# The start of an attention kernel on one core: warm-up matmuls of ones, one K half copied by DMA, odd keys turned earlier, and new numbers in its planner

## The chip, the cores and the metric

One core of one Trainium2 chip. The time is device time of one execution in microseconds (us); medians over several executions are quoted. The span of a profile is from the first to the last recorded instruction; where the same execution was timed, the time is 1.8 us above the span.

## The reference

Grouped-query attention: 8 batches, 8 query heads over 2 key/value heads, 1024 positions, head size 64, all in float32.

```python
scores = scale * np.matmul(q_group, k_group.transpose(0, 1, 3, 2))
attn = np.exp(scores - scores_max)
attn = attn / (np.sum(attn, axis=-1, keepdims=True) + 1e-08)
output[:, q_start:q_end, :, :] = np.matmul(attn, v_group)
```

## The kernel before

A job is 512 queries of one head; it has eight cells of 128 keys by 512 queries. For each cell TensorE makes a 128x512 score tile. ScalarE exponentiates most of them, two tiles at a time (`aps` to `pa`); VectorE does the rest with bit arithmetic (`dps` to `pd`). TensorE then multiplies by V. A planner (`make_plan`) simulates the engines when the program is built and fixes the order of everything. Even and odd keys sit in two halves (parity), and K is stored with zeros in the other 64 rows (side), so that one Q tile of 128 rows serves both jobs of a head. To turn a tile means to transpose it, which TensorE does here.

The first head cannot use the transposing transfers of later ones, and is prepared by hand:

```python
last_score[0] = keep_warm(WARM)              # 26 matmuls of zeros
for n, half in enumerate(halves):
    nc.scalar.copy(out=hk[:, half, 0:2, :], in_=fk[:, half])
    nc.vector.tensor_copy(out=hq[:, half], in_=...)
    turn_k(0, half)                          # two transposes: even keys
    keep_warm(2)
    ...                                      # two transposes of Q
    keep_warm(2)
...
for half in halves:
    nc.scalar.copy(out=qT[(0, 0)][:, cols], in_=tq[:, cols])
    put_k(0, 0, half)                        # VectorE: PSUM to K
def second():                                # at 0.45 us of the plan: after three scores
    turn_k(1, every)                         # four transposes: odd keys
    for side, parity in ((0, 1), (1, 0), (1, 1)):
        put_k(side, parity, every)
nc.vector.tensor_copy(out=hk[:, :, 2, :], in_=fk[:, :, 0, :])
at(SECOND, second)
```

The exponential, 411 times on ScalarE:

```python
nc.scalar.activation(out=pt[:, 0:m], in_=psum.pop(("A", n))[:, 0:m], func=AF.Exp, scale=scale)
```

The softmax here doesn't subtract the row's maximum and nothing guards it: scores larger than these inputs give would overflow.

Of the kernel before, what the change touches and what calls it, by code (L numbers as in the profile page):

```python
# [12 lines left out]
CURVE_A, CURVE_B = 0.32988085, -0.33401025  # L13

GROUP = 8
POOL_STEP = -1


def make_plan(nj, nkc):
# [5 lines left out]


    QK, PV, P1, NORM = 0.216, 0.1225, 0.603, 0.555
    EXP, AND, LINE, PRODUCT = (0.065, 0.4265), (0.20, 0.133), (0.20, 0.133), (0.16, 0.27)
    CHAIN = (AND, LINE, PRODUCT, PRODUCT)
    FROM_PE, FROM_ACT, FROM_DVE, FROM_POOL = 0.26, 0.17, 0.10, 0.15  # L30
    LIVE_A, LIVE_D, PENDING, PER_JOB, LEAD, RAMP, AHEAD, FIRST_PV = 28, 5, 16, 2, 6, 3, 0.08, 2.0
    INF = 1e9
    FIRST_LOAD, EACH_LOAD = 3.5, 4.0
    ops = []
    pe = act = dve = 0.0
    a_free, bank, obank_free = [0.0, 0.0], [0.0, 0.0], [0.0, 0.0]
# [18 lines left out]
    while normed < nj:  # L55
# [9 lines left out]
        if job_a < nj:  # L65
            t = INF
# [21 lines left out]
        for q, p, kind in ((normq, 0, "norm"), (p1q, 1, "p1"), (chainq, 2, "chain")):  # L88
            if q:
                at = q[0][0]  # L90
                if kind != "chain" or q[0][3] != POOL_STEP:
                    at = max(dve, at)
                best = min(best or (INF,), (at, p, kind, 0))
        if cur and job_d >= nj and not p1q:
# [2 lines left out]
        if kind == "qk":  # L97
            t = best[4]
            pe = t + QK
            j = job_d if arg else job_a  # L100
            cell = j * nkc + todo[j].pop(0)
            if not arg:
                if open_a is None:
                    slot = first_free(a_free)
                    a_id += 1
                    live["A"] += 1
                    open_a = {"slot": slot, "t": a_free[slot], "cells": []}
                    a_free[slot] = INF
                o = open_a
                ops.append((t, "qk", cell, "A", a_id, o["slot"], len(o["cells"])))  # L110
                o["cells"].append(cell)
                home[cell] = ("A", a_id)
                if len(o["cells"]) == 2 or not any(todo[job_a:]):
                    act = max(act, pe + FROM_PE)
                    ops.append((act, "exp", a_id, tuple(o["cells"])))
                    act += EXP[0] + EXP[1] * len(o["cells"])
                    a_free[o["slot"]] = act + FROM_ACT
                    uses[("A", a_id)] = len(o["cells"])
                    for x in o["cells"]:
                        ready[x] = act + FROM_ACT  # L120
                    open_a = None
            else:
                taken[j] += 1
                k = first_free(bank)
                bank[k] = INF
                pending += 1
                ops.append((t, "qk", cell, "D", k, 0, 0))
                p1q.append((pe + FROM_PE, cell, k))
        elif kind == "open":
            o = first_free(obank_free)  # L130
            obank[arg] = o
            obank_free[o] = INF
            open_jobs.append(arg)
            rem[arg] = list(range(nkc))
            next_job += 1
        elif kind == "pv":
            s, c = arg
            cell = s * nkc + c
            opens = len(rem[s]) == nkc
            rem[s].remove(c)  # L140
            done = not rem[s]
            ops.append((t, "pv", s, cell, opens, done, obank[s]))
            pe = t + PV
            h = home[cell]
            uses[h] -= 1
            if not uses[h]:
                live[h[0]] -= 1
            if done:
                open_jobs.remove(s)
                normq.append((pe + FROM_PE, s))  # L150
        elif kind == "norm":
            s = normq.pop(0)[1]
            ops.append((t, "norm", s))
            dve = t + NORM
            obank_free[obank[s]] = dve + FROM_DVE
            normed += 1
        elif kind == "p1":
            _, cell, k = p1q.pop(0)
            if not cur:
                d_id += 1  # L160
                live["D"] += 1
            ops.append((t, "p1", cell, k, d_id, len(cur)))
            dve = t + P1
            bank[k] = dve + FROM_DVE
            cur.append(cell)
            home[cell] = ("D", d_id)
            if len(cur) == GROUP:
                chainq.append((dve, d_id, cur, 0))
                cur = []
        elif kind == "flush":  # L170
            chainq.append((dve, d_id, cur, 0))
            cur = []
        else:
            _, g, cells, step = chainq.pop(0)
            ops.append((t, "chain", g, len(cells), step))
            end = t + CHAIN[step][0] + CHAIN[step][1] * len(cells)
            dve = end if step != POOL_STEP else dve
            if step + 1 < len(CHAIN):
                at = end + FROM_POOL if step == POOL_STEP else end
                at += FROM_DVE if step + 1 == POOL_STEP else 0.0  # L180
                chainq.insert(0, (at, g, cells, step + 1))
            else:
                pending -= len(cells)
                uses[("D", g)] = len(cells)
                for x in cells:
                    ready[x] = dve + FROM_DVE
# [4 lines left out]
def kernel(  # L191
# [25 lines left out]
    NQS = QBS // 128  # L217
    E1 = D + 1
    PIECE = 256
    WARM = 26  # L220
    SECOND = 0.45
    CAST_GAP = 3.0
    scale = 1.0 / math.sqrt(D)
    bits_scale = 128.0 * scale * math.log2(math.e)
    bits_bias = 128.0 * 127.0
# [4 lines left out]

    jobs = [(b, h, side) for b in range(B) for h in range(H) for side in range(2)]
    plan = make_plan(len(jobs), NKC)

    const_pool = ctx.enter_context(tc.tile_pool(name="constp", bufs=1))
    scr_pool = ctx.enter_context(
# [19 lines left out]
    apools, dbanks, obanks = psum_pools("aps", 2), psum_pools("dps", 2), psum_pools("ops", 2)  # L255

    blank = const_pool.tile([128, 128], BF16)
    nc.vector.memset(blank, 0.0)  # L258
    ident = const_pool.tile([128, 128], BF16)
    make_identity(nc, ident)  # L260
    vsets, ksets = [], []
# [11 lines left out]

    def at(t, f, *args):
        events.append((t, len(events), f, args))

    qT = {}
    kT = {}
# [49 lines left out]
    def first_loads():  # L328
# [46 lines left out]
        for n, half in enumerate(halves):  # L375
            nc.scalar.copy(out=hk[:, half, 0:2, :], in_=fk[:, half])  # L376
            nc.vector.tensor_copy(
                out=hq[:, half], in_=fq[:, half].rearrange("p c two d -> p c (two d)")
            )
            turn_k(0, half)  # L380
            keep_warm(2)
            for c in range(NHC)[half]:
                nc.tensor.transpose(tq[:, c * 128 : (c + 1) * 128], hq[:, c, :], ident)  # L383
            keep_warm(2)
            if n == 0:
                cast(("q", 0, 2), q[0, 2])
        for half in halves:
            cols = slice(half.start * 128, half.stop * 128)
            nc.scalar.copy(out=qT[(0, 0)][:, cols], in_=tq[:, cols])  # L389
            put_k(0, 0, half)  # L390
        def second():
            every = slice(0, NHC)
            turn_k(1, every)
            for side, parity in ((0, 1), (1, 0), (1, 1)):
                put_k(side, parity, every)

        nc.vector.tensor_copy(out=hk[:, :, 2, :], in_=fk[:, :, 0, :])
        at(SECOND, second)

    p_of = {}  # L400
    psum = {}
# [43 lines left out]

    def exp_curve(g, m, step):
        pd = groups[g][:, 0:m]
        if step == 0:
            z = tmp_pool.tile([128, GROUP, QBS], U16, name="z")[:, 0:m]
            temps[g] = [z]  # L450
            nc.vector.tensor_scalar(  # L451
                out=z, in0=pd, scalar1=0x7F, scalar2=None, op0=ALU.bitwise_and
            )
        elif step == 1:
            y = tmp_pool.tile([128, GROUP, QBS], FP16, name="y")[:, 0:m]
            temps[g].append(y)
            nc.vector.tensor_scalar(  # L457
                out=y,
                in0=temps[g][0],
                scalar1=CURVE_A / 128.0,  # L460
# [3 lines left out]
            )  # L464
        elif step == 2:
            z, y = temps[g]
            nc.vector.tensor_tensor(out=y, in0=z, in1=y, op=ALU.mult)  # L467
        else:
            y = temps.pop(g)[1]
            groups.pop(g)  # L470
            nc.vector.tensor_tensor(out=pd, in0=pd, in1=y, op=ALU.add)  # L471

    def output_mms(s, cell, opens, closes, bk):
        b, h, side = jobs[s]
# [13 lines left out]
    def normalise(s):  # L488
# [1 line left out]
        o = ops_of.pop(s)  # L490
        rec = recip_pool.tile([128, NQS], FP32, name="rec")
        nc.vector.reciprocal(out=rec, in_=o[:, :, D])  # L492
        if side == 0:
            stage[(b, h)] = ostage_pool.tile([128, NQS, 2, D], FP32, name="ost")
        nc.vector.tensor_tensor(  # L495
            out=stage[(b, h)][:, :, side, :],
# [9 lines left out]
            in_=stage[(b, h)][:, :, sides],  # L506
        )

    first_use = {}
    run = {"qk": score, "exp": exps, "p1": exp_bits, "chain": exp_curve,  # L510
           "pv": output_mms, "norm": normalise}
    for op in plan:
        if op[1] == "qk":
            first_use.setdefault(op[2] // (2 * NKC), op[0])
        elif op[1] == "norm":
            b, h, side = jobs[op[2]]
            if op[2] >= len(jobs) - 2:
                at(op[0] + 0.01, put_out, b, h, slice(side, side + 1))
            elif side:
                at(op[0] + 1.5, put_out, b, h, slice(0, 2))  # L520
        at(op[0], run[op[1]], *op[2:])

# [4 lines left out]
    for b in range(B):  # L527
        for h in range(H):
# [8 lines left out]
            if h % HPG == 0:  # L537
# [4 lines left out]
                    at(th - 11.0 - 15.0 * spare + n, transpose_k, b, g, n)  # L542
                for side in range(2):
                    for parity in range(2):
                        at(th - 6.0 - 9.0 * spare, place_k, b, g, side, parity)
                for two in range(2):
                    at(th - 4.0 - 8.0 * spare + two, place_v, b, g, two)
    casts.sort(key=lambda e: e[0])
    latest = 1e9
    for n in reversed(range(len(casts))):  # L550
# [3 lines left out]
    for t, key, src in casts:  # L554
        t = max(t, soonest)
        soonest = t + 2.0
        at(t, cast, key, src)
    with tc.manual_schedule():
        first_loads()
        for _, _, f, args in sorted(events, key=lambda e: e[:2]):  # L560
# [31 lines left out]
```

## Time and profile before

| | before |
|---|---|
| median time, 3 executions | 393.41 us (393.38 to 393.47) |
| the profiled execution: span, and its own time | 393.7 us, 395.51 us |
| ScalarE busy | 380.7 us (97%) |
| fourth exponential starts | 13.30 us |
| last exponential ends; last normalisation ends; span ends | 388.33; 389.81; 393.70 us |

The prediction below shows the lines that carry this and how to read them. In the timeline a row is start, duration, engine, line, what was written from what, how many were merged, and in brackets the idle time before and what ended it.

### The profile page before, as it was taken

The numbers are of one execution on the slowest core, as the hardware profiler recorded it, in microseconds if no ns is written. First come the engines' busy times: TensorE is split into PE (matmuls) and PEld (weight loads), VectorE is DVE, ScalarE is ACT, GpSimd is POOL, SyncE is SP. The second block draws the span as 40 slices with busy tenths as digits, with TensorE's granted clock in tenths as the row PEclk, the third lists the DMA queues.
The fourth block names the chain that finished last, engine by engine and source line by source line (L and its number), as shares of the span: only waits on it lengthen the run. The fifth ranks groups of instructions, "written<-read, shape, count | busy, mean of one in ns | idle before, by whom it ended". The sixth has DMA issues, their size and how long they took to land.

```text
span 393.7 us, 12506 instructions
## 1 busy us (share of the span) xinstructions
PE 371.0 (94%) x5166; PEld 234.3 (60%) x5166; DVE 366.2 (93%) x573; ACT 380.7 (97%) x416; POOL 107.1 (27%) x184
## 2 busy tenths in 40 slices
PE   7989999999999999999999999999999999999995
PEld 5435556566666566566566566566556556556664
DVE  3799999999999999999999999999999999999992
ACT  4799999999999999999999999999999999999994
POOL 4285241413205032141413305032331416000000
PEclk9999999999999999999999999999999999999999
DMA  7499995756959559394665868468595658520113
GB/s 120 87 169 203 140 142 101 148 80 126 156 100 148 109 111 148 91 156 86 123 107 116 143 117 132 105 115 134 103 133 105 130 87 148 101 72 28 55 55 82
DMA packets 101992, 45.39 MB, mean 115 GB/s; under 512 B 66256, under 2 KB 99536, under 8 KB 100688
## 3 DMA queue, kind: packets, MB, share of 16 engines
q0 software_dynamic: 21600, 17.05, 34.9%
q1 hardware_dynamic: 79792, 27.29, 30.5%
q8 instruction: 40, 0.66, 0.7%
q10 hardware_dynamic: 544, 0.26, 0.2%
q14 instruction: 16, 0.13, 0.1%
HBM read 25.17 MB, written 27.00 MB: 133 GB/s over the span
## 4 chain that ended last, share of the span: by engine, by line
ACT 81%; PE 11%; issue 6%; DMA 1%; DVE 0%
ACT pa L427 80%; PE aps L416 5%; PE ops L479 4%; PE dps L416 2%; DMA fk<-in_k_dram 1%; DVE kset L350 0%; PE dps L341 0%; ACT qT L389 0%; PE ops L368 0%; PE dps L383 0%; DVE ost L495 0%; ACT hk L376 0%; DVE rec L492 0%
## 5 line engine op out<-in xcount | busy, mean ns | idle before, releaser
L427 ACT ACTIVATE pa<-aps 128x1024 bf16<-128x1024 f32 x411 | 378.0, 1064 | 3.9 <-PE aps L416 3.8
L416 PE MATMUL aps<-qT,kset 128*128 128x512 bf16 x822 | 245.8, 380 | 15.8 <-ACT pa L427 13.8
L479 PEld LDWEIGHTS <-pa 128*128 128x128 bf16 x3288 | 137.6, 98 | 61.1 <-issue 1.1
L479 PE MATMUL ops<-vset,pa 128*128 128x65 bf16 x3288 | 149.1, 194 | 0.0
L436 DVE TENSOR_SCALAR pd<-dps 128x512 uint16<-128x512 f32 x202 | 130.9, 682 | 3.7 <-PE dps L416 3.1
L416 PEld LDWEIGHTS <-kset 128*128 128x128 bf16 x1024 | 82.6, 98 | 73.4 <-issue 37.4
L286 POOL DMA_DIRECT2D scr_q<-in_q_dram x63 | 34.4, 545 | 201.5 <-PE aps L416 152.2
L416 PE MATMUL dps<-qT,kset 128*128 128x512 bf16 x202 | 71.4, 383 | 1.2 <-DVE kset L350 0.9
L495 DVE TENSOR_TENSOR ost<-ops,rec 128x256 f32<-128x256 f32 x128 | 54.3, 424 | 4.4
L471 DVE TENSOR_TENSOR pd<-pd,y 128x4096 uint16<-128x4096 uint16 (+1 forms) x26 | 57.8, 2224 | 0.3
L467 DVE TENSOR_TENSOR y<-z,y 128x4096 f16<-128x4096 uint16 (+1 forms) x26 | 57.7, 2220 | 0.1
L479 PEld LDWEIGHTS <-pd 128*128 128x128 bf16 x808 | 36.5, 97 | 18.3 <-DVE pd L471 0.6
L479 PE MATMUL ops<-vset,pd 128*128 128x65 bf16 x808 | 41.3, 193 | 0.0
L306 POOL DMA_DIRECT2D kset<-kT x60 | 34.5, 584 | 1.4 <-issue 0.4
L457 DVE TENSOR_SCALAR y<-z 128x4096 f16<-128x4096 uint16 (+1 forms) x26 | 31.5, 1210 | 0.0
L451 DVE TENSOR_SCALAR z<-pd 128x4096 uint16<-128x4096 uint16 (+1 forms) x26 | 31.3, 1202 | 0.0
L492 DVE RECIPROCAL rec<-ops 128x4 f32<-128x4 f32 x128 | 22.6, 176 | 9.0 <-PE ops L479 7.7
L319 POOL DMA_DIRECT2D vset<-in_v_dram x32 | 26.4, 831 | 2.1 <-issue 1.9
L286 POOL DMA_DIRECT2D scr_k<-in_k_dram x15 | 8.1, 540 | 28.1 <-PE aps L416 22.2
L368 PE MATMUL ops<-blank 128*128 128x128 bf16 x34 | 4.6, 312 | 1.0 <-DVE blank L258 1.0
L368 PEld LDWEIGHTS <-blank 128*128 128x128 bf16 x34 | 3.7, 148 | 1.0 <-DVE blank L258 1.0
L350 DVE COPY kset<-dps 64x512 bf16<-64x512 bf16 (+1 forms) x5 | 1.7, 365 | 2.8 <-PE dps L341 2.7
(19 smaller groups left out, 12.6 us busy)
## 6 DMA issues: line engine op xcount, KB each, us to landing
out_dram<-ost SPq DMA_DIRECT2D x63, 256.0 KB, 3.2
scr_q<-in_q_dram POOLq DMA_DIRECT2D x63, 128.0 KB, 3.2
kset<-kT POOLq DMA_DIRECT2D x60, 64.0 KB, 3.4
vset<-in_v_dram POOLq DMA_DIRECT2D x32, 64.0 KB, 4.9
qT<-scr_q SPq DMA_TRANSPOSE x126, 4.0
scr_k<-in_k_dram POOLq DMA_DIRECT2D x15, 128.0 KB, 3.2
kset<-kset POOLq DMA_DIRECT2D x6, 128.0 KB, 4.9
kT<-scr_k SPq DMA_TRANSPOSE x30, 4.0
```

Source lines behind the costliest of these rows:

```text
L286: dma = nc.gpsimd.dma_start(out=scr.rearrange("(p f) -> p f", f=1024), in_=src.rearrange("(p s) d -> p (s d)", s=1024 // D),)
L306: nc.gpsimd.dma_start(out=ksets[b % 2][side * D : (side + 1) * D, g, side, parity * HALF : (parity + 1) * HALF], in_=kT[(b, g)][parity * D ...
L319: nc.gpsimd.dma_start(out=vsets[b % 2][:, g, two * NHC : (two + 1) * NHC, 0:D], in_=v[b, g].rearrange("(c p two) d -> two p c d", p=128, t ...
L416: last_score[0] = nc.tensor.matmul(dst, lhsT=ksets[b % 2][:, h // HPG, side, c * 128 : (c + 1) * 128], rhs=qT[(b, h)], start=True, stop=Tr ...
L427: nc.scalar.activation(out=pt[:, 0:m], in_=psum.pop(("A", n))[:, 0:m], func=AF.Exp, scale=scale)
L436: nc.vector.tensor_scalar(out=groups[g][:, slot], in0=psum.pop(cell), scalar1=bits_scale, scalar2=bits_bias, op0=ALU.mult, op1=ALU.add,)
L451: nc.vector.tensor_scalar(out=z, in0=pd, scalar1=0x7F, scalar2=None, op0=ALU.bitwise_and)
L457: nc.vector.tensor_scalar(out=y, in0=temps[g][0], scalar1=CURVE_A / 128.0, scalar2=CURVE_B, op0=ALU.mult, op1=ALU.add,)
L467: nc.vector.tensor_tensor(out=y, in0=z, in1=y, op=ALU.mult)
L471: nc.vector.tensor_tensor(out=pd, in0=pd, in1=y, op=ALU.add)
L479: nc.tensor.matmul(ops_of[s][:, qs, :], lhsT=p_of[cell][:, qs * 128 : (qs + 1) * 128], rhs=vsets[b % 2][:, h // HPG, c, :], start=opens an ...
L495: nc.vector.tensor_tensor(out=stage[(b, h)][:, :, side, :], in0=o[:, :, 0:D], in1=rec.unsqueeze(2).to_broadcast([128, NQS, D]), op=ALU.mult,)
```

## The change

The intent: keep TensorE busy until the first scores so that its clock is up by then; turn the odd keys while Q is copied, so that nothing interrupts the scores; and fill the zero-padded second half of K by one transfer instead of two VectorE copies. The planner's numbers change with it.

```diff
-LIVE_A, LIVE_D, PENDING, PER_JOB, LEAD, RAMP, AHEAD, FIRST_PV = 28, 5, 16, 2, 6, 3, 0.08, 2.0
+LIVE_A, LIVE_D, PENDING, PER_JOB, LEAD, RAMP, AHEAD, FIRST_PV = 28, 5, 16, 3, 6, 6, 0.08, 2.0
-FIRST_LOAD, EACH_LOAD = 3.5, 4.0
+FIRST_LOAD, EACH_LOAD = 4.5, 4.2
...
-    WARM = 26
+    WARM = 30
-    nc.vector.memset(blank, 0.0)
+    nc.vector.memset(blank, 1.0)
...
+            nc.vector.tensor_copy(out=hk[:, half, 2, :], in_=fk[:, half, 0, :])
             turn_k(0, half)
...
-        for half in halves:
+        for copy, half in zip((nc.scalar.copy, nc.vector.tensor_copy), halves):
             cols = slice(half.start * 128, half.stop * 128)
-            nc.scalar.copy(out=qT[(0, 0)][:, cols], in_=tq[:, cols])
             put_k(0, 0, half)
-        def second():
-            ...
-        at(SECOND, second)
+            copy(out=qT[(0, 0)][:, cols], in_=tq[:, cols])
+        turn_k(1, slice(0, NHC))
+        last_score[0] = keep_warm(4)
+        put_k(0, 1, slice(0, NHC))
+        nc.gpsimd.dma_start(out=ksets[0][hi, 0, 1, :], in_=ksets[0][lo, 0, 0, :])
```

Cut: an option to run steps of the curve on GpSimd (`POOL_STEPS`), which stays empty, the bookkeeping for heads whose second job finishes first, and the move of one `keep_warm(2)` (after the second half of Q there are no ones any more).

More of the change, by code (lines that the diff above doesn't have):

```diff
@@ L15 @@
 GROUP = 8
-POOL_STEP = -1
+POOL_STEPS = ()
 def make_plan(nj, nkc):
     QK, PV, P1, NORM = 0.216, 0.1225, 0.603, 0.555
-    EXP, AND, LINE, PRODUCT = (0.065, 0.4265), (0.20, 0.133), (0.20, 0.133), (0.16, 0.27)
-    CHAIN = (AND, LINE, PRODUCT, PRODUCT)
+    EXP = (0.065, 0.4265)
+    CHAIN = ((0.20, 0.133), (0.20, 0.133), (0.16, 0.27), (0.16, 0.27))
     FROM_PE, FROM_ACT, FROM_DVE, FROM_POOL = 0.26, 0.17, 0.10, 0.15
-    LIVE_A, LIVE_D, PENDING, PER_JOB, LEAD, RAMP, AHEAD, FIRST_PV = 28, 5, 16, 2, 6, 3, 0.08, 2.0
+    LIVE_A, LIVE_D, PENDING, PER_JOB, LEAD, RAMP, AHEAD, FIRST_PV = 28, 5, 16, 3, 6, 6, 0.08, 2.0
     INF = 1e9
-    FIRST_LOAD, EACH_LOAD = 3.5, 4.0
+    FIRST_LOAD, EACH_LOAD = 4.5, 4.2
     ops = []
@@ L90, in make_plan @@
                 at = q[0][0]
-                if kind != "chain" or q[0][3] != POOL_STEP:
+                if kind != "chain" or q[0][3] not in POOL_STEPS:
                     at = max(dve, at)
@@ L167, in make_plan @@
             if len(cur) == GROUP:
-                chainq.append((dve, d_id, cur, 0))
+                chainq.append((dve + FROM_DVE * (0 in POOL_STEPS), d_id, cur, 0))
                 cur = []
         elif kind == "flush":
-            chainq.append((dve, d_id, cur, 0))
+            chainq.append((dve + FROM_DVE * (0 in POOL_STEPS), d_id, cur, 0))
             cur = []
@@ L176, in make_plan @@
             end = t + CHAIN[step][0] + CHAIN[step][1] * len(cells)
-            dve = end if step != POOL_STEP else dve
+            dve = end if step not in POOL_STEPS else dve
             if step + 1 < len(CHAIN):
-                at = end + FROM_POOL if step == POOL_STEP else end
-                at += FROM_DVE if step + 1 == POOL_STEP else 0.0
+                at = end
+                if (step in POOL_STEPS) != (step + 1 in POOL_STEPS):
+                    at += FROM_POOL if step in POOL_STEPS else FROM_DVE
                 chainq.insert(0, (at, g, cells, step + 1))
@@ L219 @@
     PIECE = 256
-    WARM = 26
-    SECOND = 0.45
+    WARM = 30
     CAST_GAP = 3.0
+    POOL_DMA = 1.0
     scale = 1.0 / math.sqrt(D)
@@ L232 @@
     plan = make_plan(len(jobs), NKC)
+    starts = {}
+    for op in plan:
+        if op[1] == "chain" and op[4] in POOL_STEPS:
+            starts.setdefault(op[2], []).append(op[0])
+    chains = sorted((min(t), max(t)) for t in starts.values())
     const_pool = ctx.enter_context(tc.tile_pool(name="constp", bufs=1))
@@ L275, in at, with at_pool @@
         events.append((t, len(events), f, args))
+    def at_pool(t, f, *args):
+        for first, last in chains:
+            if first - POOL_DMA < t < last:
+                t = last + 0.01
+        at(t, f, *args)
     qT = {}
@@ L383, in first_loads @@
                 nc.tensor.transpose(tq[:, c * 128 : (c + 1) * 128], hq[:, c, :], ident)
-            keep_warm(2)
             if n == 0:
+                keep_warm(2)
                 cast(("q", 0, 2), q[0, 2])
-        for half in halves:
+        for copy, half in zip((nc.scalar.copy, nc.vector.tensor_copy), halves):
             cols = slice(half.start * 128, half.stop * 128)
-            nc.scalar.copy(out=qT[(0, 0)][:, cols], in_=tq[:, cols])
             put_k(0, 0, half)
-        def second():
-            every = slice(0, NHC)
-            turn_k(1, every)
-            for side, parity in ((0, 1), (1, 0), (1, 1)):
-                put_k(side, parity, every)
-        nc.vector.tensor_copy(out=hk[:, :, 2, :], in_=fk[:, :, 0, :])
-        at(SECOND, second)
+            copy(out=qT[(0, 0)][:, cols], in_=tq[:, cols])
[3 more added lines that the diff above has]
+        nc.gpsimd.dma_start(out=ksets[0][hi, 0, 1, :], in_=ksets[0][lo, 0, 0, :])
     p_of = {}
@@ L447, in exp_curve @@
         pd = groups[g][:, 0:m]
+        eng = nc.gpsimd if step in POOL_STEPS else nc.vector
         if step == 0:
@@ L450, in exp_curve @@
             temps[g] = [z]
-            nc.vector.tensor_scalar(
+            eng.tensor_scalar(
                 out=z, in0=pd, scalar1=0x7F, scalar2=None, op0=ALU.bitwise_and
@@ L456, in exp_curve @@
             temps[g].append(y)
-            nc.vector.tensor_scalar(
+            eng.tensor_scalar(
                 out=y,
@@ L466, in exp_curve @@
             z, y = temps[g]
-            nc.vector.tensor_tensor(out=y, in0=z, in1=y, op=ALU.mult)
+            eng.tensor_tensor(out=y, in0=z, in1=y, op=ALU.mult)
         else:
@@ L470, in exp_curve @@
             groups.pop(g)
-            nc.vector.tensor_tensor(out=pd, in0=pd, in1=y, op=ALU.add)
+            eng.tensor_tensor(out=pd, in0=pd, in1=y, op=ALU.add)
     def output_mms(s, cell, opens, closes, bk):
@@ L492, in normalise @@
         nc.vector.reciprocal(out=rec, in_=o[:, :, D])
-        if side == 0:
+        if (b, h) not in stage:
             stage[(b, h)] = ostage_pool.tile([128, NQS, 2, D], FP32, name="ost")
@@ L507, in put_out @@
         )
-    first_use = {}
+    first_use, ended = {}, {}
     run = {"qk": score, "exp": exps, "p1": exp_bits, "chain": exp_curve,
@@ L518 @@
                 at(op[0] + 0.01, put_out, b, h, slice(side, side + 1))
-            elif side:
+            elif ended.setdefault(op[2] // 2, op[2]) != op[2]:
                 at(op[0] + 1.5, put_out, b, h, slice(0, 2))
@@ L544 @@
                     for parity in range(2):
-                        at(th - 6.0 - 9.0 * spare, place_k, b, g, side, parity)
+                        at_pool(th - 6.0 - 9.0 * spare, place_k, b, g, side, parity)
                 for two in range(2):
-                    at(th - 4.0 - 8.0 * spare + two, place_v, b, g, two)
+                    at_pool(th - 4.0 - 8.0 * spare + two, place_v, b, g, two)
     casts.sort(key=lambda e: e[0])
@@ L556 @@
         soonest = t + 2.0
-        at(t, cast, key, src)
+        at_pool(t, cast, key, src)
     with tc.manual_schedule():
```

## The prediction

> **What bounds the kernel now.** I read the page's busy shares first, then the groups, then who waited for ScalarE, and last the timeline of the first 14 us and of the end.
>
> ```profile
> PE 371.0 (94%) x5166; PEld 234.3 (60%) x5166; DVE 366.2 (93%) x573; ACT 380.7 (97%) x416; POOL 107.1 (27%) x184
> ...
> L427 ACT ACTIVATE pa<-aps 128x1024 bf16<-128x1024 f32 x411 | 378.0, 1064 | 3.9 <-PE aps L416 3.8
> ```
>
> ScalarE is the bound: 411 exponentials of two score tiles each take 378.0 us of a 393.7 us span, one per 378.0/411 = 0.920 us (the 1064 ns of one overlaps its neighbour). The other column matters more: in the whole run ScalarE sat idle before these only 3.9 us. The waits view, limited to the first 14 us, says that the whole 3.8 us of it are four waits there:
>
> ```profile
> ACT pa L427 <- PE aps L416: 3.8, 4, 1.7
> ```
>
> So between 13.3 us and the end there is nothing to win on ScalarE; what can move is the start (until the exponentials run back to back) and the tail after the last of them. The timeline of ScalarE from 7 to 14 us shows the four waits (start, duration, line, tiles, idle before and its releaser):
>
> ```profile
> 7.53 1.02 ACT L427 ACTIVATE pa<-aps 128x1024 bf16<-128x1024 f32 x1 [1.10 <-PE aps L416]
> 8.81 1.02 ACT L427 ACTIVATE pa<-aps 128x1024 bf16<-128x1024 f32 x1 [0.26 <-PE aps L416]
> 11.58 1.02 ACT L427 ACTIVATE pa<-aps 128x1024 bf16<-128x1024 f32 x1 [1.75 <-PE aps L416]
> 13.30 1.02 ACT L427 ACTIVATE pa<-aps 128x1024 bf16<-128x1024 f32 x1 [0.70 <-PE aps L416]
> ```
>
> At 0.92 each the fourth should start at 7.53 + 3 x 0.92 = 10.29; it starts at 13.30, 3.01 us late. The timeline of all engines says why:
>
> ```profile
> 1.00 2.95 PE L368 MATMUL ops<-blank 128*128 128x128 bf16 x26 [1.00 <-DVE blank L258]
> ...
> 6.48 1.44 PE L416 MATMUL aps<-qT,kset 128*128 128x512 bf16 x3 [0.52 <-ACT qT L389]
> ...
> 7.71 0.63 PE L341 MATMUL dps<-ident,hk 128*128 128x128 bf16 x4
> ...
> 8.38 1.22 DVE L350 COPY kset<-dps 64x512 bf16<-64x512 bf16 x3 [2.35 <-PE dps L341]
> ...
> 9.66 1.03 PE L416 MATMUL dps<-qT,kset 128*128 128x512 bf16 x2 [0.89 <-DVE kset L350]
> ...
> 13.83 0.59 PE L416 MATMUL aps<-qT,kset 128*128 128x512 bf16 x2
> ```
>
> Two causes. First, TensorE runs at half rate: three score matmuls take 1.44 us at 6.48 (starts 0.43 us apart, one lasts 0.63), whereas two take 0.59 at 13.83 (0.22 apart, 0.38 each). The switch falls at about 13.7. The warm-up matmuls of zeros from 1.00 to 3.95 did not bring it. Second, the odd keys are turned after the third score (7.71) and three VectorE copies (8.38 to 9.60) follow; TensorE waits 0.89 us for them before the fifth score.
>
> **What the Trainium skill says.** "TensorE: Matmul & The Clock Gate", Part 1: the array starts at half clock, and one window of about 3.4 us of sustained work releases it; the window runs freely. The trace agrees with the two rates (0.43 and 0.22 us for 512 columns). With the switch near 13.7 the window before it would be 10.3 to 13.7, all busy, and the one before that holds the 0.89 us gap. That fits, but the trace cannot say whether zeros failed to count or the gaps (0.39 us at 3.68, 0.52 at 5.96) did. The same page, Part 4, says that a transpose does not count as busy in the same way; there are twelve in the start, and no line here tests it. "DMA: Bandwidth & Descriptors", Anatomy of one DMA, gives about 2 us of fixed cost to a GpSimd-issued transfer; this trace has a better number, the copies of one K tile into another (128 KB, L326): 3.2 to 3.4 us from issue to landing in the calm stretch at 19 us, 4.9 median. No page bears on the scheduler's plan.
>
> **The change part by part.**
>
> Ones for zeros, 30 for 26, and four more at the end. The memset goes from 64 words to 128 elements: the 64x512 memsets take 0.485 us, the 64 wide one 0.11, so about 0.05 us more; TensorE starts at 1.05. Thirty starts at 2.64/25 = 0.106 us end at 4.22, past 4.07 where the first transpose starts now. While cold that delays the train of transposes by 0.15 us; in exchange the 0.39 us gap is gone.
>
> Odd keys turned while Q is copied. The order of instructions on TensorE in the changed program has the four transposes before the first score, not after the third, then four matmuls of ones. They wait for VectorE, because they write the tile that it is reading for the even keys. Cold: second half of K turned by 5.48, two copies 5.52 to 6.0 (0.48 us as now), the four transposes from 6.05, ones until 6.9, so the first score at about 6.9. Warm by 5 us: K turned by 5.25, copies to 5.77, transposes and ones to 6.3. Q is copied meanwhile: ScalarE half (0.36 us) and then VectorE half (0.27, waits for ScalarE in the built program), 0.7 us against 0.65 now, so it gains nothing but ends before the ones do. First score 6.3 to 6.9 against 6.48.
>
> One copy in place of three. VectorE does one 64x512 copy (0.42 us), ending 6.75 to 7.1. The fifth and sixth scores wait for that alone, and it is done when they come: the 0.89 us wait goes.
>
> The DMA. The zero-padded half for the second job is filled by one 128 KB transfer, issued when that copy ends, at 6.8 to 7.2; plus 3.2 us it lands at 10.0 to 10.4. The ninth score (job 1) waits for it, and TensorE is in order: eight output matmuls and the two scores of the fourth exponential stand behind. Warm, from landing to that exponential: 0.07 to wake, 0.22 the ninth score, 0.24 eight output matmuls, 0.22 and 0.38 the pair, 0.04 to wake ScalarE: 1.17. So the fourth exponential starts at 11.2 to 11.6, say 11.4, against 13.30: 1.9 us gained, with a new idle of about 1 us in front of it.
>
> The plan (third cell per job for VectorE, slower lead, later loads). I ran the planner of both: 411 exponentials and 202 VectorE cells in each, so no work moves between engines. Its own model puts the gaps between exponentials at a few hundredths, before and after. At the end it has two cells' output matmuls after the last exponential instead of most of two jobs': from its end to the end of the last normalisation 1.56 us before, 1.23 after (the trace has 1.48 before: 388.33 to 389.81). That is 0.33 us off the tail. Loads: the second head is needed about 12.2, its transposes land by 10; fine.
>
> Sum: 393.4 - 1.9 - 0.3 = 391.2, and I put back 0.2 for TensorE catching up behind the late ninth score: 391.4.
>
> **The rivals.**
> (a) TensorE stays cold until about 10 or later. For it: 34 such matmuls did nothing in the kernel before, and transposes may not count. Against it: the gaps are closed now and the data are ones. Then the first exponential is at 8.0, the ninth score at 10.45, its followers at 0.43 us, and the fourth exponential at about 12.4 to 12.8; with the tail, 392.5 to 393.2.
> (b) The DMA lands late, as in the median of 4.9 us: the fourth exponential at 13.1, all of the gain at the start gone; 393.1. Against it: around 7 us the other transfers land in 2.9 to 3.3.
> (c) The DMA does not gate, because it lands in 2 us and the clock is up by 4.5: fourth exponential at 10.0, 389.9. The shortest landing of any K write here is 1.8 us, but of half the bytes.
> (d) The new plan starves ScalarE later (a K load for head 4 lands about 29 us, near its first use). Up to 1 us; the planner's margins elsewhere (reuse of Q, K and V buffers) are 11 us or more.
>
> **Range and chances.** I weigh (a) 30%, (b) 12%, (c) 8%, (d) on top of any 10%, the main line the rest: mean about 391.8. Range 390.3 to 393.3. Even with no idle at all at the start the gain could not pass 3.0 + 0.6 + 0.3 us, 1% of the time, so over 2% faster is out of reach; over 2% slower would need 8 us of new waits on ScalarE.
>
> **What would show it.** Right: score matmuls of 0.38 us from 7 us on; four ScalarE waits shrunk to one of about 1 us before the fourth exponential, with TensorE idle until the K-to-K transfer lands near 10; VectorE's K copies at two small and one large; the last normalisation 1.15 us after the last exponential. Wrong: 0.63 us scores after 8 us, a fourth exponential after 12, a transfer that lands before 9 or after 11, or any ScalarE wait above 0.3 us after 15 us.

## The result

The changed kernel took 392.9 us (median of 4, 392.56 to 393.49); the kernel before 393.39 on the same occasion. The ratio is 0.999, interval 0.9973 to 1.0007. The prediction's main line was 391.4 and its mean over all cases 391.8, so 1.6 to 2.0 us to gain; 0.5 us came, and the interval does not tell that from nothing.

Yet the start in the profile of after looks better than predicted. ScalarE from 5 us to 60 us:

```profile
5.37 0.37 ACT L404 COPY qT<-dps 128x256 bf16<-128x256 bf16 x1 [0.63 <-PE dps L397]
6.76 2.85 ACT L437 ACTIVATE pa<-aps 128x1024 bf16<-128x1024 f32 x3 [1.01 <-PE aps L426]
10.26 49.97 ACT L437 ACTIVATE pa<-aps 128x1024 bf16<-128x1024 f32 x54 [0.65 <-PE aps L426]
```

The fourth exponential starts at 10.26, where 11.4 was predicted and the profile before had 13.30. The timeline of all engines shows the steps of the change:

```profile
1.06 3.38 PE L381 MATMUL ops<-blank 128*128 128x128 bf16 x30 [1.06 <-DVE blank L264]
...
5.68 0.38 PE L354 MATMUL dps<-ident,hk 128*128 128x128 bf16 x4 [0.35 <-DVE kset L363]
...
6.10 0.42 DVE L363 COPY kset<-dps 64x512 bf16<-64x512 bf16 x1
6.13 1.03 PE L426 MATMUL aps<-qT,kset 128*128 128x512 bf16 x3
...
6.81 0.55 POOL L408 DMA_DIRECT2D kset<-kset  x1 [1.55 <-DVE kset L363]
...
9.16 0.39 PE L426 MATMUL dps<-qT,kset 128*128 128x512 bf16 x1 [0.73 <-DMA kset<-kset]
```

Scores run at full rate from the first (each of these three lasts 0.38 us in the trace; the record of one more between them is missing), the odd keys are turned before them, and TensorE's one long wait is for the transfer, as foreseen; the transfer landed 2.3 us after its issue. The span is 390.8 against 393.7, 2.9 us less. So two numbers disagree: 2.9 us between the two profiles, 0.5 us between the timed executions. And inside the profile of after a piece is missing: the fourth exponential comes 3.04 us earlier, the end of the last one only 1.98 us (386.35 against 388.33). Between them 1.06 us were lost. Its group:

```profile
L437 ACT ACTIVATE pa<-aps 128x1024 bf16<-128x1024 f32 x411 | 378.2, 1068 | 2.4 <-PE aps L426 1.7
L426 PE MATMUL aps<-qT,kset 128*128 128x512 bf16 x731 | 224.3, 378 | 16.1 <-ACT pa L437 14.6
```

2.4 us of idle, of which 1.7 are waits for scores. What is left, 0.7 us, is idle that no other engine ended. (The matmul count is 731 of 822 because some records are missing.)

### The profile page after: what moved, and what is told of

Read it like the earlier page. It is cut to its first block, busy times and chain, and to the rows that moved or that the text cites. A ratio compares the mean times of both kernels' runs of the same rounds, so it can differ in the third digit from the quotient of the medians.

```text
span 390.8 us, 12423 instructions
## 1 busy us (share of the span) xinstructions
PE 363.8 (93%) x5081; PEld 233.9 (60%) x5172; DVE 366.4 (94%) x573; ACT 380.6 (97%) x415; POOL 111.1 (28%) x185
## 4 chain that ended last, share of the span: by engine, by line
ACT 74%; PE 19%; issue 5%; DMA 1%; DVE 0%
ACT pa L437 74%; PE aps L426 8%; PE ops L490 6%; PE dps L426 3%; PE ops L381 1%; DMA kset<-kset 1%; DVE kset L363 0%; PE dps L354 0%; DVE ost L506 0%; DVE rec L503 0%; DVE blank L264 0%; PE dps L397 0%
## 5 line engine op out<-in xcount | busy, mean ns | idle before, releaser
L426 PE MATMUL aps<-qT,kset 128*128 128x512 bf16 x731 | 224.3, 378 | 16.1 <-ACT pa L437 14.6
L490 PE MATMUL ops<-vset,pa 128*128 128x65 bf16 x3288 | 147.3, 194 | 2.9
L299 POOL DMA_DIRECT2D scr_q<-in_q_dram x63 | 35.8, 568 | 197.6 <-PE aps L426 139.1
L426 PE MATMUL dps<-qT,kset 128*128 128x512 bf16 x202 | 70.0, 378 | 1.8 <-DMA kset<-kset 0.7
L490 PEld LDWEIGHTS <-pd 128*128 128x128 bf16 x808 | 37.3, 97 | 21.1 <-DVE ost L506 0.5
L332 POOL DMA_DIRECT2D vset<-in_v_dram x32 | 28.8, 905 | 3.0 <-issue 3.0
L339 POOL DMA_DIRECT2D kset<-kset x6 | 3.1, 529 | 0.0
```

The costliest lines, as they stand in the source:

```text
L299: dma = nc.gpsimd.dma_start(out=scr.rearrange("(p f) -> p f", f=1024), in_=src.rearrange("(p s) d -> p (s d)", s=1024 // D),)
L332: nc.gpsimd.dma_start(out=vsets[b % 2][:, g, two * NHC : (two + 1) * NHC, 0:D], in_=v[b, g].rearrange("(c p two) d -> two p c d", p=128, t ...
L426: last_score[0] = nc.tensor.matmul(dst, lhsT=ksets[b % 2][:, h // HPG, side, c * 128 : (c + 1) * 128], rhs=qT[(b, h)], start=True, stop=Tr ...
L490: nc.tensor.matmul(ops_of[s][:, qs, :], lhsT=p_of[cell][:, qs * 128 : (qs + 1) * 128], rhs=vsets[b % 2][:, h // HPG, c, :], start=opens an ...
```

## The experiments

Two questions: was the profile of before a usual execution, and where do the 1.06 us in the middle go? Every run was profiled and timed in five rounds beside the kernel before. For each I took five numbers from its trace; the third, fourth and fifth column add up to the span:

| run | full clock from | fifth exponential starts | from there to the end of the last | from there to the end of the span | span | median time |
|---|---|---|---|---|---|---|
| before, profile first read | 13.70 | 14.47 | 373.87 | 5.37 | 393.70 | (395.51) |
| e1 before again | 5.50 | 11.93 | 373.85 | 5.34 | 391.12 | 393.15 |
| after, first profile | 4.55 | 11.25 | 375.11 | 4.49 | 390.84 | 392.9 |
| e2 after again | 3.97 | 11.19 | 375.11 | 4.49 | 390.79 | 392.61 |
| e3 old start, new plan | 5.05 | 11.74 | 374.26 | 4.47 | 390.48 | 392.00 |
| e4 new start, old plan | 4.73 | 11.44 | 375.08 | 5.38 | 391.90 | 394.19 |
| e5 after, one more ScalarE instruction | 6.51 | 11.88 | 373.83 | 4.50 | 390.21 | 391.89 |
| e6 after, two more | 5.51 | 12.07 | 375.72 | 4.49 | 392.28 | 393.07 |
| e7 before, one more | 6.00 | 11.97 | 375.20 | 5.35 | 392.52 | 394.32 |
| e8 after, VectorE copies for the DMA | 6.31 | 11.11 | 375.07 | 4.48 | 390.66 | 392.27 |
| e9 after, one more and VectorE copies | 4.60 | 11.12 | 373.84 | 4.49 | 389.45 | 391.27 |
| e10 after with zeros | 6.15 | 12.10 | 375.10 | 4.48 | 391.68 | 393.24 |
| e11 before with ones | 6.43 | 11.97 | 374.62 | 5.36 | 391.94 | 393.27 |
| e12 after, gaps open | 4.68 | 11.35 | 375.92 | 4.48 | 391.75 | 393.43 |

"Full clock from" is the start of the full-rate entry in the trace's clock record, counted from the first instruction; the lengths of the matmuls agree with it (0.63 to 0.38 us for 512 columns). 406 spacings of 0.918 us and a last exponential of 1.07 us make 373.8 us, so that is the fourth column when nothing is lost. The execution that was profiled is not always a middle one: e4's was its fastest (393.67 us), e6's its slowest (394.05).

The third column depends on the second. The change's start has its fifth exponential at 11.19 to 11.44 where the clock was up by 4.73, and at 11.88 to 12.10 where it was up at 5.51 or later. At like clocks (e1 and e6, e7 and e10, e11 and e5) it is 0.14 and 0.13 us later than the old start, and 0.09 us earlier.

### e1: the kernel before, again

No edit.

> The unchanged kernel, once more with its own profile. Theory 1 (the profile of before that the prediction read was an exceptional execution: 395.51 us, cold TensorE until 13.70 us, while the timed ones took 393.4): here the time is 393.2 to 393.5, the profiled span about 391.5 if it falls in a usual execution, 512-column scores reach 0.38 us before 10.5 us, the fourth exponential starts near 11.2 instead of 13.30. Theory 2 (the start of that profile is the usual one, and the 2 us come from the profiling): span again 393.7, scores of 0.63 until about 13.7, fourth exponential at 13.3.

Measured: 393.15 us, just under the range, span 391.1. ScalarE, from 5 us to 60 us:

```profile
7.03 1.94 ACT L427 ACTIVATE pa<-aps 128x1024 bf16<-128x1024 f32 x2 [0.68 <-PE aps L416]
9.82 1.02 ACT L427 ACTIVATE pa<-aps 128x1024 bf16<-128x1024 f32 x1 [0.85 <-PE aps L416]
11.01 49.71 ACT L427 ACTIVATE pa<-aps 128x1024 bf16<-128x1024 f32 x54 [0.16 <-PE aps L416]
```

and TensorE of the same kernel (all engines, 3.5 to 16 us):

```profile
6.40 0.81 PE L416 MATMUL aps<-qT,kset 128*128 128x512 bf16 x3 [0.62 <-ACT qT L389]
7.05 0.39 PE L341 MATMUL dps<-ident,hk 128*128 128x128 bf16 x4
...
8.75 0.61 PE L416 MATMUL dps<-qT,kset 128*128 128x512 bf16 x2 [1.10 <-DVE kset L350]
```

Three scores take 0.81 us where the first profile had 1.44: with the same zeros and the same gaps the clock was up at 5.50, not at 13.70. The wait for the odd keys is there in both. So the fourth exponential of a usual execution starts at 11.01, and 2.3 of the 3.0 us by which the prediction found it late are not lost in it. Theory 1 holds.

What differed between the two executions can be worked out from the clock records. In all fourteen traces the first full-rate entry lasts 378.88, 382.29 or 385.71 us; these are 3.41 us apart, so the switches lie on a grid of 3.41 us, and where the grid lies against the first instruction differs from execution to execution. In the first profile it lies at 0.05, 3.46, 6.87, 10.29 and 13.70, and the four stretches between hold 0.95, 0.64, 0.88 and 0.00 us without a matmul record. In the other thirteen traces the clock is up at the end of the first stretch that holds less than 0.6 us of that (at most 0.53, in e11); each stretch before it held 1.38 us or more (time before the first instruction included). So the old start with its gaps is late when the grid falls badly. Between 3.46 and 6.87 the changed start idles some 0.1 to 0.4 us (e10 and after), so on the grid of the first profile its clock should be up at 6.87; that is an estimate, and no trace of it met such a grid.

How rare is the late case? In the three batches the kernel before was timed 33 times for comparison and six times as e1: 33 times 392.53 to 393.57 us, and six times 395.28 to 395.95, nothing between. The first profile's 395.51 lies in the upper group. That every execution of that group has a late clock is inferred from this one trace.

These executions are in the ratios below: one of the 11 of before in each of the first two batches, three in that of e9 to e12. Without them, by plain means, the ratio of e9 is 0.9953, of e10 and e11 1.0005, of e12 1.0009; those of e2 to e8 rise by 0.0005 to 0.0006.

### e2: the changed kernel, again

No edit.

> The changed kernel once more. Theory 1: 392.6 to 393.5, fourth exponential near 10.3, warm between 4.5 and 7.9 us whatever the phase, and again about 1.1 us of lateness of the exponentials between 20 us and the end (sum of start-to-start spacings above 0.918). If that lateness was chance in one execution it is under 0.3 us here.

Measured: 392.61 us, ratio to before 0.9993 (0.9974 to 1.0012). The fourth column is 375.11 again, 1.26 above e1: the lateness in the middle is no chance. The clock was up at 3.97, earlier than the 4.5 that I had expected as the least.

### e3 and e4: start and plan apart

e3 is the change without its start; e4 is the change with the old planner numbers.

```diff
# e4
-LIVE_A, LIVE_D, PENDING, PER_JOB, LEAD, RAMP, AHEAD, FIRST_PV = 28, 5, 16, 3, 6, 6, 0.08, 2.0
+LIVE_A, LIVE_D, PENDING, PER_JOB, LEAD, RAMP, AHEAD, FIRST_PV = 28, 5, 16, 2, 6, 3, 0.08, 2.0
-FIRST_LOAD, EACH_LOAD = 4.5, 4.2
+FIRST_LOAD, EACH_LOAD = 3.5, 4.0
# e3: the same four lines the other way round, in the kernel before (with the bookkeeping of after)
```

> The start of before (zeros, 26, odd keys after the third score, no DMA) with the planner numbers of after. If the new plan costs 1.1 us in the middle and saves 0.3 at the tail: 394.0 to 394.4. If the plan costs nothing (rival: the lateness in the profile of after is chance or comes from the start): 392.9 to 393.3.

> The start of after with the planner numbers of before (PER_JOB 2, RAMP 3, loads 3.5 and 4.0). If the plan costs 1.1 us: 391.7 to 392.3, better than both, and under 0.3 us of lateness after 20 us. If the plan costs nothing: 392.9 to 393.4. Head 1 is needed 0.7 us earlier than in after, so a wait for its Q of up to 1 us is possible.

Measured: e3 392.00 us, 0.9972 of before (0.9954 to 0.9990); e4 394.19 us, 1.0037 (1.0013 to 1.0060). My theory was that the new plan costs the time in the middle. It falls. Both times lie outside both forecasts: e3 is faster than either, e4 slower. The plan is the good part, and the new start brings the loss. Column four says where: 375.08 with the new start and the old plan, 374.26 with the old start and the new plan. (The 0.4 us of e3 above 373.85 are one wait, for the K of the fifth head; see e12.) Column five belongs to the plan: 4.47 against 5.38.

How can a start of 7 us cost time evenly over the next 340? The spacings of the exponentials in the trace of after stand out at 45.4, 104.4, 163.3, 222.4, 281.4 and 340.4 us: 58.9 us apart, which is 64 exponentials, and in e4, with another plan, within 0.3 us of the same places. (One more of 1.16 us, at 180.0, is in every trace with the new plan and in none with the old, e5 and e9 too, so it belongs to the plan.) From about the 28th on, each exponential has two records in ScalarE's stream, a wait on a semaphore and the ACTIVATE, so 64 exponentials are 128 records. Counting the records of ScalarE, the first being number 0:

```
                          record 63   191    319    447    575    703
after             what is it   ACT    ACT    ACT    ACT    ACT    ACT
                  since the record before, us
                             0.37   0.34   0.34   0.35   0.34   0.34
                  spacing    1.22   1.20   1.18   1.11   1.19   1.26
e1 before         what is it  wait   wait   wait   wait   wait   wait
                  spacing    0.92   0.92   1.00   0.92   0.92   0.93
```

Elsewhere an ACTIVATE follows its wait by 0.07 us. In the changed kernel record 63 and each 128th after it is late. (The next ACTIVATE also stands 0.3 to 0.4 us after its wait, but only because that wait came early: its spacing is 0.9.) In the kernel before, these records are semaphore waits. A wait stands some 0.85 us after the start of the previous ACTIVATE at any place, and at these places too (0.75 to 0.86): the previous exponential runs meanwhile, and a pause in that time costs nothing. The change took one instruction out of the stream (the second half of Q, given to VectorE), everything moved up by one, and the place fell on the ACTIVATE. The trace also has an 8192-byte transfer on the queue it labels "instruction" 0.7 to 2.0 us after each of the six late starts (8192 bytes over 128 records are 64 bytes each). Such a transfer follows these places in e1 and e5 too (by 0.03 to 1.5 us), where no exponential is late, and it starts after the late exponential, so it is not what that one waited for. That this place is where a new block of instructions is needed is argued from the count, not shown.

### e5, e6 and e7: one instruction more, or two

If this is right, an idle instruction anywhere ahead moves the place back.

```diff
 last_score[0] = keep_warm(WARM)
+idle = first_pool.tile([128, 4], BF16, name="idle")
+for i in range(1):                     # 2 in e6; e7 is this edit in the kernel before
+    nc.scalar.copy(out=idle[:, i : i + 1], in_=blank[:, i : i + 1])
```

> The changed kernel with one more instruction on ScalarE: a copy of one column, while ScalarE waits for its first load. Theory 3: the changed kernel has one instruction fewer in ScalarE's stream (its half of the Q copy went to VectorE), so every 128th instruction boundary falls on an exponential and no longer on the semaphore wait ahead of it, and costs about 0.25 us, six times; in its trace these are the exponentials number 41, 105, 169, 233, 297, 361. One more instruction puts the boundary back on the wait: 391.3 to 391.8, no start-to-start spacing of 1.15 us or more at these places, lateness between 50 and 400 us under 0.3 us. Rival (the lateness comes of something else in the new start, such as the DMA or VectorE's part): 392.6 to 392.9, the gaps stay.

> The changed kernel with two more such copies on ScalarE. Theory 3: the boundary is on an exponential again (number 40, 104 and so on, one earlier): 392.5 to 393.0, six gaps of about 1.2 us, one exponential earlier than in the changed kernel. Rival (any idle work in front helps, or the stream's length does not matter): as with one more.

> The kernel before with one more copy on ScalarE. Theory 3: the six gaps appear here too, 1.0 to 1.2 us slower than before: 394.0 to 394.4. Rival (the gaps come of the new start): 392.9 to 393.3, no gaps.

Measured: e5 391.89 us, 0.9966 of before (0.9943 to 0.9989); e6 393.07 us, 1.0004 (0.9982 to 1.0026); e7 394.32 us, 1.0051 (1.0020 to 1.0081). The times of e5 and e6 are 0.1 us above their ranges, that of e7 is inside. One more, and column four falls from 375.11 to 373.83; two more, and the six gaps are back, each one exponential earlier (number 40 instead of 41, and so on); one more in the kernel before, and they appear there, 375.20 against 373.85. (In e6's 375.72, 0.5 us are the wait for K again.) The exponentials around the second place, in the timeline of after and of e5 (three each):

```profile
102.26 3.14 ACT L437 ACTIVATE pa<-aps 128x1024 bf16<-128x1024 f32 x3
```

```profile
102.65 2.92 ACT L440 ACTIVATE pa<-aps 128x1024 bf16<-128x1024 f32 x3
```

3.14 us for three against 2.92, with no idle shown in brackets: the profile's idle column cannot be relied on for this, since consecutive exponentials overlap by about 0.1 us and hide part of the pause. Only counting spacings showed it. So where the stream stands decides: theory 3 foretold the sign and the places in all three, and the rivals, that the DMA or VectorE's part brings the loss or that any idle work helps, fall. (Two of e7's six times are 396.73 and 397.04, its upper group, and are in its ratio; without the upper groups it is 1.0034.)

### e8: VectorE copies in place of the transfer

```diff
-nc.gpsimd.dma_start(out=ksets[0][hi, 0, 1, :], in_=ksets[0][lo, 0, 0, :])
+for parity in range(2):
+    put_k(1, parity, slice(0, NHC))
```

> The changed kernel with the second half of the zero-padded K written by two VectorE copies (about 0.8 us, ending near 7.4 us) in place of the DMA that lands at 9.1 to 9.4. If the DMA is what the fourth exponential waits for: it starts at about 9.5 instead of 10.2 and the time falls by 0.6 to 0.8 us, to 391.8 to 392.0 (the six gaps stay). If the wait is hidden or something else takes its place (the ninth score waits for a PSUM bank that VectorE frees): under 0.3 us, 392.4 to 392.6.

Measured: 392.27 us, 0.9978 of before (0.9958 to 0.9999). The wait before the fourth exponential is gone:

```profile
7.35 7.53 ACT L438 ACTIVATE pa<-aps 128x1024 bf16<-128x1024 f32 x8 [1.01 <-PE aps L427]
```

In this execution the clock came up late (6.31), the first exponential starts at 7.35, and still the fifth starts at 11.11; in e5, with the transfer and the clock at 6.51, it starts at 11.88. So the transfer costs 0.77 us where the two are comparable. The six gaps stay (375.07), as they should. The fourth exponential starts at 10.13, not at the 9.5 expected. Between medians the gain is 0.34 us over e2, less than the 0.6 to 0.8 expected and between the two forecasts; e2 and e8 were not run in the same batch, but all five times of e8 (at most 392.46) lie below all ten of the change (at least 392.56).

### e9: both repairs

The edits of e5 and e8 together.

> The changed kernel with both repairs: one more idle instruction on ScalarE, and two VectorE copies in place of the DMA. If the two gains are separate: 0.7 to 1.0 us from the first and 0.5 to 0.7 from the second, 391.0 to 391.5, fourth exponential near 10.1 for a clock switch at 6.3, no gap at 64-exponential spacing. If they overlap: 391.6 or more.

Measured: 391.27 us against 393.21 for before in the same rounds, 0.9933 (0.9901 to 0.9965). It is the fastest of all and its fourth column is 373.84. It beats both kernels: it has the third column of e8 and the fourth of e5. Against the median of e2 it wins 1.34 us, where e5 wins 0.72 and e8 0.34; these come from three batches.

```profile
L441 ACT ACTIVATE pa<-aps 128x1024 bf16<-128x1024 f32 x411 | 377.6, 1069 | 1.1 <-PE aps L430 1.0
```

Of ScalarE's idle before exponentials only the wait for the first is left, 1.0 us.

### e10, e11 and e12: zeros, ones and gaps

```diff
# e10: the changed kernel
-nc.vector.memset(blank, 1.0)
+nc.vector.memset(blank, 0.0)
# e11: the kernel before, the reverse
# e12: the changed kernel
-WARM = 30      keep_warm(4)
+WARM = 22      keep_warm(1)
```

> The changed kernel with zeros in the warm-up operand. The old start with zeros has had full clock at 5.0 to 6.0 us in three traces and at 13.70 in one. If the data do not matter: as the changed kernel, 392.5 to 393.5, full clock before 8 us. If ones are what brings the clock up: scores of 0.63 us until 10 us or later, 394 to 395.5.

> The kernel before with ones in the warm-up operand. If the data do not matter: as before, 392.6 to 393.5, now and then a run at 395 to 396 (one execution in six or so), as before has them. If ones help: no run above 393.6.

> The changed kernel with 22 warm-up matmuls in place of 30 and one in place of four after the odd keys, so that TensorE idles about 0.75 us before the first transpose. If closing the gaps is what keeps the clock switch early: now and then a run 2 us or more above the others, as before has them. If the gaps do not matter: 392.5 to 393.5 in all runs; the first transpose may start 0.15 us earlier.

Measured: e10 393.24 us (0.9985, 0.9956 to 1.0014), full clock at 6.15 with zeros; e11 393.27 us (0.9985, 0.9956 to 1.0015), full clock at 6.43 with ones; e12 393.43 us (0.9989, 0.9960 to 1.0017), full clock at 4.68 with the gap open. Ones are not needed to bring the clock up: with zeros it was up at 5.05, 5.50, 6.00 and 6.15 in four traces, and at 13.70 in the first profile. None of the eighteen runs was in an upper group. With six in 39 for the kernel before, six runs without one are no evidence (chance (33/39)^6 = 0.37), so which of ones and closed gaps, if either, removes the slow executions stays open. Over all, the change as it stands had none in its ten timed runs, and e4, with the new start, had one of 395.64, 1.45 us above its median, with 394.77 between, so it is not clear to which group it belongs.

e12 also shows a loss that the prediction named as rival (d). ScalarE's and TensorE's waits in e12 from 26 to 33 us:

```profile
PE dps L426 <- DMA kset<-kT: 0.7, 1, 0.7
ACT pa L437 <- PE aps L426: 0.6, 1, 0.6
```

The K of the fifth head lands late, and one exponential waits (spacing 1.68, 0.76 too long). The same wait is in e3 and e6 (0.2 and 0.3 us of idle, 0.45 and 0.53 of spacing), and in none of the other traces with the new plan. It depends on how the start happened to fall. (The 0.77 us of e11 in column four are two single gaps, at 17.0 and 58.7 us: one wait for a Q transfer and one for a VectorE normalisation, neither at the places above.)

## Why the prediction was wrong

Two usual executions, e1 and e2, make the account: the fifth exponential 11.93 to 11.19, -0.74 us; from it to the last 373.85 to 375.11, +1.26; the tail 5.34 to 4.49, -0.85; together -0.33 us of span. The prediction's own terms were -1.9, +0.2 and -0.3. The -0.74 is in part luck: the clock was up at 5.50 in e1 and at 3.97 in e2, and at like clocks the new start gains nothing (-0.09 to +0.14). The medians agree: e4, the new start with the old plan, is 1.30 slower than before, which is the loss in the middle alone; e5, without that loss, is 1.03 faster, of which 0.85 is the tail.

**"11.2 to 11.6, say 11.4, against 13.30: 1.9 us gained."** This step failed. The 13.30 was true of one execution, whose clock came up at 13.70; a usual one has 11.01 (e1). The sum then took 1.9 us, read in an execution of 395.51 us, off a median of 393.4 us that does not contain them. The profiled execution was 2.1 us slower than the timed ones, and the prediction did not compare the two. It asked whether zeros or gaps had kept the clock down; neither does by itself, for with both in place it was up at 5.50. Where the grid of 3.41 us fell made the gaps count (see e1); the prediction's reading of that one window, 10.3 to 13.7, was right. Rival (a)'s "34 such matmuls did nothing in the kernel before" is true of that execution alone.

**The path through the start.** In the profile of after, the mechanism was right and its sizes nearly so. First transpose predicted at 4.22, found at 4.23; first score 6.3 (warm), found 6.13; from the landing to the fourth exponential 1.10 us without the wake-up, found 1.10 (9.16 to 10.26); one ScalarE wait of about 1 us in front of it predicted, 0.65 found. The mis-sized term is the transfer: 3.2 us assumed from a later stretch of the trace, 2.3 us measured (2.3 to 2.8 in six further traces of the new start). The Trainium skill, "DMA: Bandwidth & Descriptors", Anatomy of one DMA, has a fit, 2.0 us plus bytes over 436,000 per us; for 131,072 bytes that gives an estimate of 2.3, and I set it aside for a number from a later stretch, which the prediction called calm. Two small readings were off: the "0.39 us gap" at 3.68 is one of weight loads, between matmuls it was 0.12 (3.95 to 4.07); and the prediction's own cases and chances average 392.0, not 391.8.

**"No work moves between engines"** and the sum of the plan. True, and yet the term that took back most of the gain comes from work moved between engines by the start: half of one small copy, 0.3 us, from ScalarE to VectorE. It shortened ScalarE's stream by one instruction and put a pause in front of an exponential six times, 0.21 us each (1.28 between e2 and e5). e5, e6 and e7 turn it off and on. The prediction had no term for it, and of its tests only "any ScalarE wait above 0.3 us after 15 us" was near; the waits view shows just one such, of 0.2.

**"0.33 us off the tail."** Right for what it counted: 1.48 us became 1.14 from the last exponential to the last normalisation. The tail fell by 0.85, because another transfer got out of the way as well. The last output writes, e1 and then after:

```profile
386.30 1.50 SPq L504 DMA_DIRECT2D out_dram<-ost  x3
...
386.84 0.42 DVE L495 TENSOR_TENSOR ost<-ops,rec 128x256 f32<-128x256 f32 x1
```

```profile
384.55 3.36 SPq L515 DMA_DIRECT2D out_dram<-ost  x3
...
387.08 0.42 DVE L506 TENSOR_TENSOR ost<-ops,rec 128x256 f32<-128x256 f32 x1
```

In the old plan the 256 KB write of the head before falls between the last two half-writes; in the new one it has gone out two microseconds earlier (384.55), and the last half lands 2.0 instead of 2.2 us after its issue (medians of two), with an issue of 0.37 instead of 0.49. The DMA records show it: one unbroken stretch of 2.2 us for the three writes in e1, three separate ones in after. From the end of the last normalisation to the end of the span: 3.86 us in e1, 3.34 in after.

**The rivals.** (a) and (b) did not happen in the profile of after. (c), the transfer hardly gating, came nearest for the start, at 10.0 against 10.26. (d) happened in three of nine traces with the new plan, at 0.45 to 0.76 us. The 392.9 us lies inside the prediction's range, but not for a reason that it gave: a gain that mostly was not there to win and a loss that it had no term for.

## What to carry to other kernels

Before reading a profile, compare the time of the profiled execution with the timed ones; if it differs by more than the change is worth, profile again. A difference of half a per cent in an engine that is 97% busy can come from where its instructions stand, not from what they do: sum the start-to-start spacings of the bounding instruction over stretches of the run, and if they are late at a fixed count, add or remove one idle instruction and see whether it goes. Take a change apart before judging it: this one held a good plan (e3, 0.9972), a start that gains little by itself (and 0.8 us with VectorE's copies in place of the transfer, 11.93 to 11.11 from e1 to e8), and an accident that cost 1.3.

## What the Trainium skill lacked or had wrong

- No page gives a cost to a place in ScalarE's straight-line instruction stream. The point belongs to "Runtime: NRT & Kernel Launch", Instruction fetch mechanics, which describes refills in blocks of 256 instructions and calls the cost of a block's end mostly hidden. Here each 128th record, from record 63, came 0.34 to 0.37 us after the one before it instead of 0.07 when it was an exponential, about 1.3 us in a run of 391 (e5, e6, e7). That these are refills is not shown.
- "TensorE: Matmul & The Clock Gate", Part 1, does not say whether matmuls of zeros count as work for the clock. They do: full clock at 5.05 to 6.15 us in four traces with zeros, 3.97 to 6.51 with ones. Its remark that the cold stretch varies with a free-running window fits: the same program had 5.50 and 13.70, and the switches of each trace lie on a grid of 3.41 us. Not stated is how much idle a window may hold (here windows with up to 0.53 us brought the clock up, one with 0.64 did not), nor that this can split a kernel's times into two groups, here 392.5 to 393.6 and 395.3 to 396.0 (by inference from one trace of the upper group).
- The same page, Part 4, says that transposes do not count as busy in the same way. In e10 the 3.4 us ahead of the switch at 6.15 hold ten transposes, about 1 us of TensorE's time, and the clock still came up; no run here isolates them.
- "DMA: Bandwidth & Descriptors": nothing wrong; its fit for a GpSimd-issued transfer was right within 0.5 us (2.3 to 2.8 us for 128 KB in seven traces), and a number read from a later stretch was not.
